# Seven-product multiplication with both running sums in one PSUM tile: product order, weight rounding and memory attention rearranged

## The chip, the cores and the metric

The kernel runs on one core of a Trainium2 chip. The metric is the time of one execution on the device in microseconds (us), and the lower the better. The kernel before takes 1235.52 us, the median of 3 runs (1234.53 to 1237.28).

## The reference

One layer of a hybrid streaming encoder, for a prompt of 512 tokens and a sample group of 32 tokens (544 rows in all), width 1024. The sample group attends to caches of 512 tokens. All in float32.

```
h = rms_norm(x, norm_mix)
q, k, v, xb, gb, qc = split(h @ w_in)                  # 1024 columns each
a_out = differential attention(q, k, v)                # 8 heads, two 64-wide maps each, 128-wide values
b_out = rglru(xb) * gelu(gb)                           # width-4 conv, block gates, linear recurrence
c_out = cross_attention(qc, mem_k, mem_v)              # 4 heads x 256, 256 memory tokens
gates = sigmoid(h @ w_gate + b_gate)                   # 3 x 1024 columns: ga, gb, gc
merged = gates_a * (a_out @ w_proj_a) + gates_b * (b_out @ w_proj_b) + gates_c * (c_out @ w_proj_c)
x = x + merged @ w_out
g_ff, u_ff = split(rms_norm(x, norm_ffn) @ w_ffn_in)   # 2816 columns each
x = x + (silu(g_ff) * u_ff) @ w_ffn_out
y = rms_norm(x, norm_final)
```

Before that, keys and values of the memory are made from `mem_prompt` (rms_norm and `w_mem_kv`). Besides y, the new keys and values, the memory's keys and values, and the states of the convolution and the recurrence are returned.

## The kernel before, in words

**Numbers.** Every product is made in float32r. A float32 value is split into a high part (rounded, `A(h_, src)` on ACT) and a low part (the difference, `LO` on DVE), for activations and weights alike. A product takes three passes: high weights with high and with low activations, low weights with high activations. Activations are transposed, 128 rows of the width on the partitions and 544 columns of tokens; 544 is taken as two halves of 272. PSUM is divided into two accumulators `acc` of two banks each and four `side` tiles of one bank each.

**Plain gemm** (`gemm`, L564): for 128 output rows all 8 blocks of 128 inputs, 48 matmuls of 272 columns (32 with the high weights, 16 with the low), into both banks of one `acc`.

**Seven products** (`seven`, L1820): 256 output rows and pairs of input blocks form a 2x2 scheme with seven products (A11, A12, A22, P1 to P4) instead of eight. It is used for the query of the memory attention (qc), for the gate products gb and gc, for one of ga, and for the whole first FFN matrix: 13 items of 256 columns before the FFN, 22 in it. One product is 12 matmuls of 272 columns. The running sum `a` stands in bank 0 of an `acc`, and its intermediate values are copied out by ACT between the products (`quarters`, L1869): after A11, after P2 and after P3. The next product into `a` may start when the copy has been made. The second sum `b` (P1, P4) and the single product A12 stand in a `side` tile each. The order is A11, [A22 and P4 of the item before], A12, P2, P1, P3; the last two products of an item are pending until the next item or gemm calls `flush` (L1842).

**Weights.** SP loads chunks of 1 MB, two ahead, `raw`. For the seven products, sums of weights are needed; one is added by a DMA with accumulation on POOL's queue, others by DVE (`raw<-raw`, L267). `split_blocks` (L487) issues roundings in the order of use.

**Order.** All instructions are issued at build time by a planner (`Flow`, L48). It keeps a time `fl.now` on PE and one of each engine by a cost per instruction; generators wait with `fl.get` for events and with `fl.take` for buffers, and instructions go into each engine's queue in the order of these planned times. Each engine then runs its queue in that order and waits for semaphores. The order of the weight chunks is written out by hand: `HEAD`, then `MID` (L360), where a name and a number are a chunk of 256 columns (x and g: recurrence and GeLU branch; ya, yb, yc: projections), "flush" and "cross" are marks where the main line waits, then w_out and the FFN (`FF_ORDER`).

**Memory attention** (`cross_kv` L1460, `cross` L1500): per head, keys and values come back from DRAM, go out to the result, and are split (buffers `mh`, `ml`, two each, both used by one head). Four row blocks of 128 queries each go through maximum, exponential, sum and division (`soft_rows`), then two pairs of blocks are transposed and multiplied with the values. The split queries `cq` have room for one head; a query's `t1` tile is free only when its split is made.

**Recurrence** (`x_evac` L1320, `g_evac` L1388, `scan` L1409): convolution, two gates, recurrence and GeLU, ten `L` tiles. A gate's result waits in `t1` (four of them), gb 2's and gb 3's in `L`, until its projection comes.

**Norm ahead of the FFN** (`row_norm`, L703): a sum of squares over the rows by small matmuls, an inverse root by DVE, a broadcast by small matmuls. The FFN's first products don't need it; their copies out of PSUM do.

Of the kernel before, what the change touches and what calls it, by code (L numbers as in the profile page):

```python
# [9 lines left out]
F32 = mybir.dt.float32  # L10
# [195 lines left out]
def hybrid_step(ctx: ExitStack, tc, io):  # L206
# [139 lines left out]
    def chunk(w, c, k0=0, nk=8):  # L346
# [130 lines left out]
    def split_plain(i, j):  # L477
        nk = chunks[i][1]
        for e in range(0, nk, 4):
            yield from split((i, j, e), raws[i][:, e:min(e + 4, nk), j * P:(j + 1) * P])  # L480
        ks = [((i, j, k // 4 * 4), k % 4) for k in range(nk)]
# [5 lines left out]
    def split_blocks():  # L487
# [4 lines left out]
        late = None  # L492
        for i in ORDER:
            if i == "flush":
                yield from late
                late = None
                continue
            yield from fl.get(("raw", i, 0))
            if i not in FAST:
                for j in range(2):  # L500
                    yield from split_plain(i, j)

                    if late is not None:
                        yield from late
                        late = None
# [6 lines left out]
            if late is not None:  # L512
                yield from late
# [3 lines left out]
            p2, a22, p1 = q[0], q[2], q[3]  # L517
            VT(p2, p1, q[0], OP.add)
            yield from split((i, "P2"), b4(p2))
            yield from split((i, "P1"), b4(p1))  # L520
            if aside is not None:
                yield from split((i, "P3"), b4(aside))
            else:
                yield from split((i, "A22"), b4(a22))
                VT(a22, p2, a22, OP.subtract)
                yield from split((i, "P3"), b4(a22))
            late = split_late(i, b4, a22, q[1], p2, aside)

    def split_late(i, b4, a22, a12, p2, aside):
        if aside is not None:  # L530
            yield from split((i, "A22"), b4(a22))
# [51 lines left out]
    def gemm(tiles, xh, xl, n=T, need=None):  # L583
# [18 lines left out]
        if need is None:  # L602
            for c, j, evac in tiles:
# [4 lines left out]
                yield from products(acc, c, j, [(0, b, k) for k in ks for b in range(2)], True, False)  # L608
# [46 lines left out]
    comb = tl(const, [P, 64], F32, "comb")  # L655
    onesm = tl(const, [P, P], F32, "onesm")
    ones_d = tl(const, [P, 1], F32, "ones_d")
# [7 lines left out]
    nlam = tl(const, [P, 1], F32, "nlam")  # L665
    sgn = tl(const, [P, 1], F32, "sgn")
    subg = tl(const, [P, 1], F32, "subg")
    bv = tl(const, [HEADS, REL_N], F32, "bv")
# [34 lines left out]
    def row_norm(pool, sqs, n, rb, ev, late=None):  # L703
# [6 lines left out]
        banks = len(blocks) if len(sqs) > 1 else 1  # L710
        yield from fl.take(*["side"] * banks)
# [13 lines left out]
        yield fl.when(y)  # L725
# [82 lines left out]
    def start_vecs(sp):  # L808
        yield from fl.get(("sent", 5))
        dma(comb, io["c_comb"], 32768)  # L810
# [7 lines left out]
        yield td + 1500  # L818
        yield from fl.take("side", "side")
# [29 lines left out]
    def softplus():  # L849
# [3 lines left out]
        mx, ab, ww, den, zz, z2, pl = (tl(const, [P, 8], F32, f"sp_{n}") for n in "mawdzyp")  # L853
# [80 lines left out]
    def mem_out():  # L934
# [4 lines left out]
        yield None  # L939
# [144 lines left out]
    def sample(at, p):  # L1084
# [25 lines left out]
        yield VS(cm, comb, st[:, 2:3], None, OP.mult)  # L1110
# [335 lines left out]

    def soft_rows(s_, e, free_side):
        i_st = S["cst n"] = S.get("cst n", -1) + 1
        st = S["cst"][:, 3 * i_st:3 * i_st + 3]
# [10 lines left out]
    def cross_kv(cr, h):  # L1460
        yield from fl.take("mraw", "mraw", "mh", "mh", "ml", "ml")
        res = []
        for src in (mk_d, mv_d):
            r = slot_tile(cr, [P, 2, 256], F32, "mraw")
            t = dma(r, src[h], 262144)
            res.append((r, t))
        outs = (io["o_mk"][h], io["o_mv"].rearrange("(t p) d -> p t d", p=P)[:, :, h * 256:(h + 1) * 256])
        for i, (r, t) in enumerate(res):
            yield t
            t_out = dma(outs[i], r, 262144)  # L1470
            hi = slot_tile(cr, [P, 2, 256], F32R, "mh")
            lo = slot_tile(cr, [P, 2, 256], F32R, "ml")
            yield VC(hi, r)
            t = LO(lo, r, hi)
            fl.give("mraw", max(t, t_out))
            S["mkv", h, i] = (hi, lo)
            fl.set(("mkv", h, i), t)

    def c_evac(cr, h):
        def go(c, a):  # L1480
# [3 lines left out]
            q = yield from quarters(c, new_t1, a, each, -1.0)  # L1484
# [13 lines left out]
        return lambda c, a: member("cross", go(c, a))  # L1498

    def cross(cr, h):  # L1500
# [6 lines left out]
        def rows(i):  # L1507
            yield from fl.take("ce", "side")
            s_ = side_tile()
            n = 0  # L1510
            for j in range(2):
                for a, b in ((q[j][0], mkh), (q[j][1], mkh), (q[j][0], mkl)):
# [726 lines left out]
```

## Time and profile before

| what | value |
|---|---|
| median of 3 runs | 1235.52 us |
| the profiled execution, its own time | 1239.9 us |
| its span, first to last instruction | 1238.1 us |
| TensorE matmul (PE) busy | 1182.8 us, 96% |
| VectorE (DVE) busy | 877.3 us, 71% |
| ScalarE (ACT) busy | 585.3 us, 47% |
| mean granted clock of TensorE | 0.982 |

The profile is of one execution, so sums are made against its own time. PE is the matmul engine, PEld its weight loads, which overlap. A matmul's end is modelled: one of 272 columns is shown as about 0.29 us long, while the next starts 0.125 us after it. An idle time in brackets stands in front of the instruction that waited, with the instruction that ended the wait.

### The profile page before, as it was taken

The page shows a single profiled execution, that of the slowest core. Times are in us where ns is not written, and L with a number is a line of the kernel's source. Part 1 is how long each engine was busy: PE and PEld are TensorE (multiplying, and loading weights), DVE is VectorE, ACT ScalarE, POOL GpSimd, SP SyncE. Part 2 cuts the span into 40 slices and gives each one's busy share as a digit, 9 for nine tenths or more (in the row PEclk, how much of TensorE's full clock was granted, in tenths as well). Part 3 has the DMA queues.
Part 4 walks back from the last instruction along what each step waited for, and adds up shares of the span by engine and source line. Part 5 has one row for each costly group of instructions (what it writes and reads, how often), then busy time and mean ns, then how long its engine had stood idle before and what let it go on. Part 6 is the DMA issues. An engine that isn't in the chain of part 4 may idle for free.

```text
span 1238.1 us, 23076 instructions
## 1 busy us (share of the span) xinstructions
PE 1182.8 (96%) x9200; PEld 1163.1 (94%) x9200; DVE 877.3 (71%) x1861; ACT 585.3 (47%) x1171; POOL 76.4 (6%) x145
## 2 busy tenths in 40 slices
PE   8999999999999997999999689998999999999996
PEld 8899999999999997999999689998999999999996
DVE  6886878786648885475878675578887757756755
ACT  5635454444325554353656653355455525524422
POOL 0002000000000000000111000010111011011001
PEclk9999999999999998999999899998999999999998
DMA  7682343321243443214223133343566556554322
GB/s 263 223 269 97 134 139 116 105 87 58 98 136 103 129 137 111 77 44 145 78 77 112 51 98 143 114 120 95 141 166 138 145 137 168 140 151 120 106 65 73
DMA packets 58875, 151.95 MB, mean 123 GB/s; under 512 B 6632, under 2 KB 18280, under 8 KB 52624
## 3 DMA queue, kind: packets, MB, share of 16 engines
q1 hardware_dynamic: 50560, 135.53, 32.7%
q0 software_dynamic: 8208, 14.95, 7.5%
q8 instruction: 72, 1.18, 0.4%
q14 instruction: 35, 0.29, 0.1%
HBM read 139.52 MB, written 13.68 MB: 124 GB/s over the span
## 4 chain that ended last, share of the span: by engine, by line
PE 85%; DVE 8%; ACT 4%; issue 2%; DMA 1%; SPq 0%; ACTq 0%; DVEq 0%
PE acc L327 65%; PE side L327 19%; DVE wl L267 3%; PE side L334 2%; ACT wh L254 1%; DVE raw L267 1%; DMA raw<-in_w_mem_kv 1%; ACT L L254 0%; ACT t L254 0%; DVE t L267 0%; DVE rst L267 0%; DVE fq L267 0%; DVE x L276 0%; DVE al L267 0%; ACT fq L254 0%
## 5 line engine op out<-in xcount | busy, mean ns | idle before, releaser
L254 ACT ACTIVATE wh<-raw 128x512 fp32r<-128x512 f32 (+2 forms) x357 | 234.5, 669 | 282.6 <-PE acc L327 124.6
L267 DVE TENSOR_TENSOR wl<-raw,wh 128x512 fp32r<-128x512 f32 (+2 forms) x358 | 260.7, 740 | 49.5 <-ACT wh L254 33.4
L327 PE MATMUL acc<-hh,wh 128*128 128x272 f32 x852 | 185.6, 291 | 0.0
L327 PE MATMUL acc<-hl,wh 128*128 128x272 f32 x852 | 184.3, 290 | 0.0
L327 PEld LDWEIGHTS acc<-hh,wh 128*128 128x128 f32 x852 | 137.9, 189 | 0.7 <-ACT fq L254 0.3
L327 PEld LDWEIGHTS acc<-hl,wh 128*128 128x128 f32 x852 | 137.5, 189 | 0.1
L327 PE MATMUL acc<-ah,wh 128*128 128x272 f32 x596 | 127.3, 288 | 0.0
L327 PE MATMUL acc<-al,wh 128*128 128x272 f32 x596 | 127.2, 288 | 0.0
L327 PE MATMUL acc<-hh,wl 128*128 128x272 f32 x852 | 124.7, 291 | 0.1
L327 PE MATMUL acc<-bh,wh 128*128 128x272 f32 (+2 forms) x416 | 98.1, 294 | 17.2 <-ACT t L254 14.5
L327 PEld LDWEIGHTS acc<-hh,wl 128*128 128x128 f32 x852 | 113.3, 189 | 0.6 <-DVE wl L267 0.4
L327 PE MATMUL acc<-bl,wh 128*128 128x272 f32 (+2 forms) x416 | 96.1, 289 | 0.0
L327 PEld LDWEIGHTS acc<-ah,wh 128*128 128x128 f32 x596 | 95.8, 189 | 0.0
L327 PEld LDWEIGHTS acc<-al,wh 128*128 128x128 f32 x596 | 95.5, 188 | 0.0
L327 PEld LDWEIGHTS acc<-bh,wh 128*128 128x128 f32 x416 | 71.5, 190 | 19.7 <-ACT t L254 16.7
L327 PE MATMUL acc<-ah,wl 128*128 128x272 f32 x596 | 84.1, 289 | 0.0
L327 PE MATMUL side<-hh,wh 128*128 128x272 f32 x296 | 77.7, 290 | 2.6 <-DVE t L267 2.1
L327 PEld LDWEIGHTS acc<-ah,wl 128*128 128x128 f32 x596 | 78.7, 189 | 0.0
L267 DVE TENSOR_TENSOR x<-acc,x 128x544 f32<-128x544 f32 (+2 forms) x43 | 29.3, 684 | 69.6 <-PE acc L327 69.6
L327 PE MATMUL side<-hl,wh 128*128 128x272 f32 x296 | 77.1, 288 | 0.0
L327 PEld LDWEIGHTS acc<-bl,wh 128*128 128x128 f32 x416 | 71.3, 190 | 0.0
L327 PE MATMUL acc<-bh,wl 128*128 128x272 f32 (+2 forms) x416 | 63.3, 290 | 0.0
(338 smaller groups left out, 2393.4 us busy)
## 6 DMA issues: line engine op xcount, KB each, us to landing
raw<-in_w_in SPq DMA_DIRECT2D x20, 1024.0 KB, 5.7
raw<-in_w_ffn_in SPq DMA_DIRECT2D x22, 512.0 KB, 4.3
raw<-in_w_ffn_in SPq DMA_DIRECT2D x44, 256.0 KB, 4.8
raw<-in_w_ffn_out SPq DMA_DIRECT2D x12, 768.0 KB, 4.2
raw<-in_w_mem_kv SPq DMA_DIRECT2D x7, 1024.0 KB, 6.5
fb<-in_w_ffn_in SPq DMA_DIRECT2D x22, 256.0 KB, 4.7
raw<-in_w_ffn_in POOLq DMA_DIRECT2D x22, 256.0 KB, 4.3
fb<-in_w_ffn_in POOLq DMA_DIRECT2D x22, 256.0 KB, 5.4
```

Source lines behind the costliest of these rows:

```text
L254: nc.scalar.activation(out, in_, func, scale=scale, bias=bias, accum_out=accum_out)
L267: nc.vector.tensor_tensor(out, a, b, o)
L327: nc.tensor.matmul(out, lhsT=lhsT, rhs=rhs, start=start, stop=stop, skip_group_check=shared)
L334: nc.tensor.transpose(out, in_, ident[:n, :n])
```

## The change

Six things are changed together.

1. `seven`, `flush`, `quarters`: both running sums `a` and `b` are the two banks of one `acc`, and only A12 has a `side` tile. The order is A11, [A22 of the item before], P2, [P4 of the item before], P1, P3, A12. `flush` takes one pending product or both; `gemm` calls it within its first tile after half of the high-weight matmuls and after all of them. The accumulator is given back after `b` has been read.
2. `split`: the rounding of a sum of weights is issued when its planned time of completion has come, not before. The splits come in the order of the products; without a second buffer the sum for P3 is made in P1's place.
3. `MID` has another order, and the gates' results have places by name (`HOLD`): gc 0, gc 3 and gb 1 in two new tiles `gt`, gb 2 and gb 3 in `L`.
4. Memory attention: row blocks go in pairs (one `side` tile and one maximum for two), keys and values have buffers of their own (`mhk`, `mlk`, `mhv`, `mlv`, one each), the high part is made by ACT, and the sample group has its own tile. The results o_mk and o_mv leave by copies from DRAM to DRAM, planned 150 us after the start of the attention stage.
5. yb 2 is one gemm of two tiles that takes the inputs as they come (`need`), yb 1 comes ahead of "lru", and the wait at the end of that stage is for n from 2 on.
6. `row_norm` ahead of the FFN issues its two groups of matmuls 2.5 us later each. Constants and the tiles of `softplus` go to other pools; four columns share one tile.

```diff
-    MID = [("qc", 0), ("ga", 3), ("qc", 1), ("qc", 2), ("qc", 3), ("gc", 0), ("gc", 1), "flush", "cross",
-           ("yc", 0), ("gc", 2), ("x", 0), ("yc", 1), ("gc", 3), ("yc", 2), ("g", 0), ("x", 1), ("yc", 3), "bh", ("g", 1),
-           ("gb", 0), ("x", 2), ("g", 2), ("x", 3), ("g", 3), ("gb", 1), ("gb", 2), ("gb", 3), ("yb", 2), "mh", ("yb", 3),
-           "lru", ("yb", 0), ("yb", 1)]
+    MID = [("qc", 0), ("qc", 1), ("gc", 0), ("qc", 2), ("qc", 3), ("ga", 3), ("gc", 1), ("gc", 2), "flush", "cross",
+           ("yc", 0), ("x", 0), ("gc", 3), ("yc", 1), ("g", 0), ("x", 1), ("yc", 2), ("yc", 3), "bh", ("g", 1),
+           ("x", 2), ("g", 2), ("x", 3), ("gb", 0), ("g", 3), ("gb", 1), ("gb", 2), ("gb", 3), ("yb", 2), "mh", ("yb", 3), ("yb", 1),
+           "lru", ("yb", 0)]
+    HOLD = {("gc", 0): "gt", ("gc", 3): "gt", ("gb", 1): "gt", ("gb", 2): "L", ("gb", 3): "L"}
...
     def split(name, src):
         yield from fl.take("hb", "lb")
+        if fl.when(src) > fl.now:
+            yield fl.when(src)
...
             yield from split((i, "A11"), b4(q[0]))
-            if late is not None:
-                yield from late
-            yield from split((i, "A12"), b4(q[1]))
+            if late:
+                yield from late.pop(0)
...
             VT(p2, p1, q[0], OP.add)
             yield from split((i, "P2"), b4(p2))
+            if late:
+                yield from late.pop(0)
             yield from split((i, "P1"), b4(p1))
...
+            if aside is None:
+                VT(p1, p2, a22, OP.subtract)
+            yield from split((i, "P3"), b4(p1 if aside is None else aside))
+            yield from split((i, "A12"), b4(a12))
+            late += [split((i, "A22"), b4(a22)), split_last(i, b4, a12, p2, aside)]
...
                 ks = range(chunks[c][1])
-                yield from products(acc, c, j, [(0, b, k) for k in ks for b in range(2)], True, False)
+                yield from products(acc, c, j, [(0, b, k) for k in ks[:4] for b in range(2)], True, False)
+                yield from flush(0)
+                yield from products(acc, c, j, [(0, b, k) for k in ks[4:] for b in range(2)], False, False)
+                yield from flush(1)
...
+        yield fl.now + later
         yield from fl.take(*["side"] * banks)
...
-        yield fl.when(y)
+        yield fl.when(y) + later
```

The new `seven` and `flush`:

```
        a, b = acc[:, 0, :HT], acc[:, 1, :HT]
        fl.spawn(evac(c, a, b))
        yield from product(a, c, "A11", forms, True, False)
        yield from flush(0)
        yield from fl.get(("c11", c))
        yield from product(a, c, "P2", forms, False, False)
        yield from flush(1)
        yield from fl.get(("c12", c))
        yield from product(b, c, "P1", forms, True, False)
        yield from product(a, c, "P3", forms, False, False)
        yield from fl.take("side")
        S["c", c] = c_ = side_tile()[:, :HT]
        yield from product(c_, c, "A12", forms, True, True)
        S["pending"] += [(c, a, "A22", forms), (c, b, "P4", forms)]

    def flush(*which):
        for w in which or (0, 1):
            if len(S["pending"]) == 2 - w:
                c, dst, form, forms = S["pending"].pop(0)
                yield from fl.get(*((("u3", c), ("c22", c)) if w == 0 else (("a4", c),)))
                yield from product(dst, c, form, forms, False, True)
```

The new row pairs and the buffers of memory attention:

```
            for i in range(2):
                n = 0
                for j in range(2):
                    for a, b in ((q[j][0], mkh), (q[j][1], mkh), (q[j][0], mkl)):
                        MM(s_[:, i * NMEM:(i + 1) * NMEM], a[:, (2 * qp + i) * P:(2 * qp + i + 1) * P], b[:, j], n == 0, n == 5)
                        n += 1
...
            nc.vector.tensor_reduce(st[:, 0:2], sv, AX.X, OP.max)
...
declare(mraw=1, mhk=1, mlk=1, mhv=1, mlv=1, cq=4, ce=2, ces=1, pth=1, ptl=1, ck=1, cv=1, qs=2, pts=1)
...
            if item == ("yb", 2):
                yield from gemm([(i, j, ev(2 * c + j)) for j in range(2)], xh, xl, need=lambda k: ("b", k))
                continue
```

## Rows read from the trace of the kernel before

**Rows 1.** The page's busy times by engine.
```profile
PE 1182.8 (96%) x9200; PEld 1163.1 (94%) x9200; DVE 877.3 (71%) x1861; ACT 585.3 (47%) x1171; POOL 76.4 (6%) x145
```

**Rows 2.** Busy time by stage; stretch, its length, then engines, clock, DMA.
```profile
core 0: us, PE busy (x) PEld busy (x) DVE busy (x) ACT busy (x) POOL busy (x), PEclk, DMA share, GB/s
63.00:297.00 234.00, 234.00 (x1843) 228.75 (x1842) 179.22 (x547) 107.86 (x258) 7.45 (x22) 1.00 0.39 131
...
371.00:480.00 109.00, 104.65 (x814) 102.52 (x812) 88.51 (x204) 60.33 (x140) 5.15 (x6) 0.98 0.45 131
480.00:497.00 17.00, 11.42 (x58) 9.74 (x57) 9.52 (x26) 5.03 (x13) 0.00 (x0) 0.80 0.09 34
497.00:686.00 189.00, 185.65 (x1470) 184.77 (x1469) 132.06 (x216) 99.58 (x190) 15.73 (x54) 1.00 0.28 90
686.00:748.00 62.00, 46.97 (x338) 45.64 (x337) 41.67 (x70) 39.39 (x71) 2.65 (x7) 0.89 0.23 73
...
838.00:850.00 12.00, 7.83 (x47) 7.52 (x46) 10.98 (x30) 6.08 (x11) 0.00 (x0) 0.72 0.04 7
850.00:1166.00 316.00, 311.13 (x2437) 306.31 (x2437) 227.81 (x407) 148.61 (x295) 34.94 (x40) 1.00 0.55 145
```

**Rows 3.** Waits over the whole span: us in total, times, longest.
```profile
ACT wh L254 <- DVE raw L267: 120.8, 57, 8.9
...
PE acc L327 <- ACT t L254: 16.6, 9, 8.0
```

**Rows 4.** Timeline of PE in the FFN: start us, length, engine, what.
```profile
1017.39 0.28 PE L327 MATMUL side<-hh,wh 128*128 128x272 f32 x1
...
1019.09 0.39 PE L327 MATMUL acc<-hh,bh 128*128 128x272 f32 x1
...
1025.60 1.16 PE L327 MATMUL acc<-m,wh 128*128 128x272 f32 x8
...
1030.11 0.29 PE L327 MATMUL acc<-hh,wh 128*128 128x272 f32 x1
```

**Rows 5.** Timeline of ACT in the same stretch.
```profile
1018.12 0.63 ACT L254 ACTIVATE wh<-raw 128x512 fp32r<-128x512 f32 x1 [3.88 <-DVE raw L267]
1018.66 0.38 ACT L254 ACTIVATE fq<-acc 128x272 f32<-128x272 f32 x1
...
1025.80 0.40 ACT L254 ACTIVATE t<-acc 128x272 f32<-128x272 f32 x1 [1.11 <-PE acc L327]
```

**Rows 6.** Waits of PE and PEld in the FFN, 850 to 1166 us.
```profile
PE acc L327 <- ACT t L254: 2.1, 2, 1.1
PE acc L327 <- ACT fq L254: 1.6, 3, 0.7
...
PEld acc L327 <- ACT fq L254: 4.2, 10, 0.9
PEld acc L327 <- ACT t L254: 3.3, 5, 1.3
```

**Rows 7.** Timeline of ACT, PE and DVE at the end of memory attention.
```profile
464.55 0.39 ACT L254 ACTIVATE t<-acc 128x272 f32<-128x272 f32 x1
...
465.00 0.40 PE L327 MATMUL acc<-bh,wh 128*128 128x272 f32 x1 [2.24 <-ACT t L254]
...
480.56 0.42 DVE L283 CAST mh<-mraw 128x512 fp32r<-128x512 f32 x1
```

**Rows 8.** Timeline of ACT and PE at gb 1.
```profile
703.21 0.63 ACT L254 ACTIVATE wh<-raw 128x512 fp32r<-128x512 f32 x1 [2.30 <-DVE raw L267]
...
704.73 0.60 PE L327 MATMUL acc<-bh,wh 128*128 128x272 f32 x1 [8.02 <-ACT t L254]
...
707.61 0.43 PE L327 MATMUL side<-bh,wh 128*128 128x272 f32 x1
```

**Rows 9.** Timeline of DVE in the yb projections.
```profile
759.79 0.72 DVE L276 SCALAR_TENSOR_TENSOR L<-L,acc 128x544 f32<-128x544 f32 x1 [2.21 <-PE acc L327]
```

**Rows 10.** Timeline of DVE at the norm ahead of the FFN.
```profile
846.06 0.43 DVE L267 TENSOR_TENSOR al<-fq,ah 128x272 fp32r<-128x272 f32 x1
```

More of the change, by code (lines that the diff above doesn't have):

```diff
@@ L480, in split_plain @@
             yield from split((i, j, e), raws[i][:, e:min(e + 4, nk), j * P:(j + 1) * P])
+            if between:
+                yield from between.pop(0)
+        while between:
+            yield from between.pop(0)
         ks = [((i, j, k // 4 * 4), k % 4) for k in range(nk)]
@@ L1571, in cross_sample @@
         yield from fl.get(("cq", h, 0), ("cq", h, 1))
-        yield from fl.take("ce", "side")
+        yield from fl.take("ces", "side")
         sx = side_tile()[:, :NMEM]
@@ L1674, in fast_tanh, with go @@
     def fast_tanh(br, c):
-        own = br == 1 and c >= 2
+        tag = HOLD.get(("g" + "abc"[br], c), "t1")
         def new():
-            yield from fl.take("L")
-            return l_tile(S["lr"])[:, :T]
+            if tag == "t1":
+                return (yield from new_t1())
+            yield from fl.take(tag)
+            return slot_tile(S["lr"], [P, 552], F32, "L")[:, :T] if tag == "L" else slot_tile(S["gp"], [P, T], F32, "gt")
         def bias(j):
             return bgh[:, br * 8 + 2 * c + j:br * 8 + 2 * c + j + 1]
-        def go(i, a):
+        def go(i, a, b):
             def each(g, j, cs, src):
@@ L1688, in each @@
                     yield A(g[:, cs], src, AF.Tanh, scale=0.5 if cs.start else -0.5, bias=bias(1))
-            g = yield from quarters(i, new if own else new_t1, a, each, -1.0)
+            g = yield from quarters(i, new, a, b, each, -1.0)
             t = A(g[0], g[0], AF.Tanh, scale=0.5, bias=bias(0))
@@ L1697, in go @@
                 S["gate", br, n] = g[j]
-                S["gate tag", br, n] = "L" if own else "t1"
+                S["gate tag", br, n] = tag
                 fl.set(("gate", br, n), fl.when(g[j]))
@@ L1894, in quarters @@
         yield from each(t1, 1, hi, t1[:, hi])
+        yield from fl.get(("done", c, "A12"))
+        t = VT(t0[:, lo], S["c", c], t0[:, lo], OP.add)
+        fl.give("side", t)
+        yield t
+        yield from each(t0, 0, lo, t0[:, lo])
         yield from fl.get(("done", c, "A22"))
         yield from each(t1, 1, lo, a)
-        give_acc(fl.when(t1[:, lo]))
+        fl.set(("a4", c), fl.when(t1[:, lo]))
         yield from fl.get(("done", c, "P4"))
         t = VT(t0[:, hi], b, t0[:, hi], OP.add)
-        fl.give("side", t)
+        give_acc(t)
         yield t
@@ L1914, in each @@
                     VT(g[:, cs], src, S["rb"][:, cs], OP.mult)
-            g = yield from quarters(c, new, a, each)
+            g = yield from quarters(c, new, a, b, each)
             S["fg", i, n] = g
@@ L1957, in ffn_in @@
             yield from between
-        yield from flush()
     def fo_evac(fp, i, n):
@@ L2099, in main @@
         mid = iter(MID)
-        with tc.tile_pool(name="cross", bufs=1, reuse_waits="tile") as cr:
-            S["cr"] = cr
-            declare(mraw=2, mh=2, ml=2, cq=4, ce=4, pth=1, ptl=1, ck=1, cv=1, qs=2, pts=1)
-            S["cst"] = tl(cr, [P, 60], F32, "cst")
-            ch = tl(actp, [P, KD, T], F32R, "ah")
-            cl = tl(actp, [P, KD, T], F32R, "al")
-            yield from after_attention(mid)
-            yield idle("cross")
-            yield from fl.get(*[("cs", h) for h in range(4)], *[("c", h, qp) for h in range(4) for qp in range(2)])
```

244 lines of the change are left out of this document (114 added, 130 removed).

## The prediction

> **What bounds the kernel now.** I read the page first: TensorE (PE) is busy 1182.8 of 1238.1 us [rows 1], so no other engine's load sets the time; what can be won is what PE loses. The change adds no matmul and takes none away, so the question is only which PE stalls go and which come. Next I read the table by stage [rows 2]. A stage's loss is its idle time plus (1 - clock) x length, since the granted clock has two levels, 1.2 and 2.4 GHz, and a mean of 0.80 means that part of the stretch ran at the lower one. That gives: 371-480 us 4.35 + 2.2, 480-497 us 5.58 + 3.4 (memory attention, with the query and gate products, 15.5 together); 497-686 us 3.35, 686-748 us 15.03 + 6.8 (recurrence and gates, 25.2 together); 838-850 us 4.17 + 3.4 (second norm, 7.5); 850-1166 us 4.87 (FFN). The reader is to see that these sum to 53, that the pairs' stage (63-297 us) loses nothing, and that three short stretches hold most of it.
>
> The waits [rows 3] name the culprit: PE waits longest for ScalarE (ACT) copies, and ACT itself stands 120.8 us, 57 times, in roundings of weights whose sum VectorE (DVE) has not made. A copy issued behind such a rounding is late, as one shows [rows 4 to 5]: the first product of an item ends at 1017.39, its copy starts only at 1018.66, behind the rounding of 1018.12 that came after 3.88 us of waiting for the sum. The copy ends at 1019.04 and PE goes on at 1019.09. An undisturbed copy stands beside it: product over at 1025.60, copy 1025.80 to 1026.20. So a copy that nothing delays holds PE up 0.20 + 0.40 + 0.05 = 0.65 us if PE has nothing else to do.
>
> **The change, part by part.** A product is 1.50 us: 1025.60 to 1030.11 are three of them [rows 4].
>
> *Order of the seven products, sums in two banks of one tile.* There are 35 such items, 22 of them in the FFN. In the old order the first copy (after A11) has three products as cover, 4.5 us; the second (after P2) and third (after P3) have one, 1.5 us. In the new order the first has one (A22 of the item before), the second two (P4, P1), the third two (A12, next A11): cover of 1.5, 3.0, 3.0. One thin spot instead of two. But where no item is pending, P2 follows A11 with no cover at all, 0.65 us each: qc 0, gc 3, gb 0, gb 1 and the first item of each of three FFN groups. Every later product stands behind P2 in PE's queue, so these are paid in full.
>
> *Rounding only when the sum is made.* The planner now issues the rounding at the time it reckons the sum ready, so copies get in front. In the FFN this should remove nearly every wait of PE for ACT. Its size lies between 3.7 us (the matmuls' waits, 2.1 + 1.6) and 7.5 us (the weight loads' waits for the same copies, 4.2 + 3.3) [rows 6]; I take 6.0, above the middle, because a stall also costs the overlap with the matmul before it (1.50 / 12 = 0.125 apart, shown as 0.28 long [rows 4]). Less two uncovered starts at 0.65 (the third is in the norm's stage): **FFN -4.7** (from -6.2 to 0, the latter if ACT is held as before and the thinner cover eats the rest).
>
> *Memory attention.* Two things hold PE. At 465.00 it waits 2.24 us for a copy which ACT makes at 464.55, behind the query splits: the gate's tile waited for a t1 buffer that the last head's query still held. And in the tail, 480-497 us, PE has only the last head's chain; it starts with the keys' rounding at 480.56, which could not begin while the head before still had its buffers [rows 7]. After the change keys and values have buffers of their own, the keys' free after the second row pair; gc 0 and gc 3 have tiles of their own; and gc 2's 7 x 1.50 = 10.5 us of products stand ahead of "cross", where 9.0 us are lost now. I let 6.0 of the 15.5 remain, because the chain row sums, transposes, products stays serial: -9.5, and +0.65 for qc 0: **-8.8** (from -14.9 to +0.65, the latter if the tail only starts later). Row pairs make 16 row maxima into 8, and the keys' and values' rounding goes from DVE to ACT; both lie beside PE work (ACT 60.33, DVE 88.51 of 109 us [rows 2]), priced at nothing. If that cover went, one rounding (0.63 [rows 5]) would stand before a head's first row, at most 4 x 0.63 in all.
>
> *Gates and recurrence.* The largest single wait is 8.02 us at 704.73: gb 1's second product waits for the first copy [rows 8]. ACT was in a line of recurrence work and then stood 2.30 us in a weight rounding at 703.21; and the copy needed a t1 buffer that the last GeLU tiles held. Now gb 1 has a tile that is free, its rounding no longer blocks, and gb 0's 10.5 us lie between the last x and the last g product. But ACT's recurrence work is all still there, and gb 0 meets it with no cover. Between "all 25.2 stay" and "all go" no row decides; I take half, -12.6, plus three uncovered starts (gc 3, gb 0, gb 1), +1.95: **-10.6** (from -23.2 to +16.8, the third rival).
>
> *yb 2 as one two-tile gemm.* gb 3's item is still pending and holds one of two accumulators, and it is flushed only in yb 3. So yb 2's two halves and yb 3 share the other one, and PE waits twice for an evacuation that another accumulator hides now: 0.20 + 0.72 + 0.05 each, the 0.72 from the DVE evacuation [rows 9]: **+1.9** (from 0, if gb 3's DVE work fits, to +1.9).
>
> *The norm's matmuls 2.5 us later, twice.* PE would not wait for the sum of squares. But the input that the first FFN product needs, al from fq, is itself written only at 846.06 [rows 10], and the new order asks for the later forms (P2, P1) right after A11, uncovered. So most of the 7.5 stays: **-1.0** (from -7.5 to +1.3, two uncovered waits).
>
> *Priced at nothing:* the outputs of memory keys and values now leave in the pairs' stage, eight transfers on SP's queue in front of weight loads. PE idles 0.00 of 234 us there with DMA engines at 0.39 [rows 2], so weights arrive early. Comb, the small constants and softplus's tiles only change pools. If the cover were gone, a late weight tile would show as waits of PE for DMA in 200-297 us, where there is none.
>
> **Sum.** -4.7 - 8.8 - 10.6 + 1.9 - 1.0 = -23.2 us. The profiled execution took 1239.9 us (span 1238.1 and 1.8 around it), 4.4 above the median of 1235.5; there the change should give 1216.7, at the median 1212.3.
>
> **A rule that speaks against it.** The FFN has some fifteen waits of up to 1.3 us [rows 6] with the granted clock at 1.00 throughout [rows 2], so short stalls of this kind have not lowered it.
> The Trainium skill (page "TensorE: Matmul & The Clock Gate", section "A second HAM failure mode: psum-queue depth-cycling") says that PE idling briefly and often between groups of matmuls as it goes through PSUM banks can be enough to swing its clock between both levels; the uncovered starts would be such idles. By the trace the sum stays; by the rule it is the fifth case below.
>
> **The rivals.**
> 1. *The stalls move rather than go.* The tail of memory attention starts 10.5 us later with half its length won (-4 instead of -9.5), the recurrence stage gives 4 instead of 12.6, the rest as forecast: 1212.3 + 5.5 + 8.6 = 1226. For it: the order is fixed by a planner whose costs have missed stalls of 8 us. Against: the largest two each have a named buffer that the change frees.
> 2. *All goes:* cross -13, gates -20 + 2, FFN -6.2: 1212.3 - 4 - 7.4 - 1.5 = 1199. Against it: the serial chains stay.
> 3. *Slower: gb 0 behind the last x product.* Its first copy stands uncovered behind ACT's recurrence line. If PE waits 8.0 us there and the clock falls as it did (6.8), and gb 1's wait stays, the stage loses 14.8 more instead of 12.6 less, +16.8 with the starts: 1212.3 + 10.6 + 16.8 = 1240. It decides from a loss in gb 0 and gb 1 together of some 23 us more than forecast. For it: ACT is busy 39.39 of 62 us there [rows 2]. Against: ACT stood idle behind weight sums in that very line.
> 4. *The rounding rule does nothing,* since it goes by planned, not real time: FFN 0 and 5 us more in the two earlier stages, 1222.
> 5. *The clock falls at uncovered starts:* a product at the lower level took 2.88 us (704.73 to 707.61 [rows 8]) against 1.50, so 7 x 1.4 more: 1222.
>
> **How the numbers follow.** Forecast 0.52 (1203 to 1223), first rival 0.19, second 0.12, slower 0.11, fourth 0.03, fifth 0.03. The likeliest gives 1212. Leaving out about a tenth on either side, the range is 1196 to 1237: below lies the unlikely half of the second case, above the slower one. A difference of 0.2% (2.5 us) is what can be told from none here. Faster than that: all but the slower case and the end of the first, 0.84; within 0.05; slower 0.11.
>
> **What would show it.** Right: ACT's waits for weight sums fall from 120.8 to below 40; PE's waits for ACT in the FFN below 2 us except about 0.65 at each group's start; no wait at gb 1 over 2 us; the stretch from the last gate's flush to yc 0 below 10 us; two waits of about 1 us around yb 2. Wrong: PE waiting for the first copy in most items (the cover of 1.5 us too thin), several us at gb 0, a tail of 15 us after gc 2, or PE waiting for weights, which would mean that the later roundings starve it.

## The result and the profile after

The changed kernel takes 1277.15 us (median of 4 runs, 1275.03 to 1277.68) against 1235.74 in the runs beside it: ratio 1.0331, interval 1.0313 to 1.0349. It is slower by 41 us; I had forecast 1212 and a range that ended at 1237.

Busy times of the page, after. The amount of PE work is the same (x9200); PE is busy 14.7 us longer than in [rows 1], in a span that is 37.8 us longer.

```profile
PE 1197.5 (94%) x9200; PEld 1170.9 (92%) x9200; DVE 876.5 (69%) x1828; ACT 591.6 (46%) x1180; POOL 75.7 (6%) x145
```

Busy time by stage, after, in the columns of [rows 2].

```profile
370.00:498.00 128.00, 124.32 (x982) 121.98 (x981) 100.26 (x210) 76.96 (x175) 5.15 (x6) 1.00 0.38 112
498.00:690.00 192.00, 184.70 (x1440) 182.64 (x1440) 138.34 (x223) 110.47 (x206) 15.12 (x55) 0.99 0.26 85
690.00:748.00 58.00, 48.74 (x374) 47.04 (x374) 36.47 (x61) 26.46 (x49) 2.54 (x6) 1.00 0.28 96
...
823.00:835.00 12.00, 7.47 (x37) 6.41 (x37) 10.63 (x29) 6.36 (x12) 0.00 (x0) 0.74 0.00 0
835.00:1240.00 405.00, 367.35 (x2732) 356.24 (x2732) 253.81 (x444) 159.43 (x312) 34.94 (x40) 0.97 0.45 120
```

Memory attention now loses 3.7 us, where [rows 2] gave 15.5, and the recurrence and gates lose 18.5 (7.3 + 1.9 and 9.3 + 0) instead of 25.2. Counted in matmuls these two stretches won less than the 18.5 us by which the losses differ: 2796 in 378 us, where the rows of before have 2680 in 377, which at 0.125 us each is 13.5 us. The FFN is the news: 37.65 us idle in 405 and a clock of 0.97, where the rows of before had 4.87 in 316 and 1.00. One row stands for the split, the write of the input that the first FFN product needs, in DVE's timeline after; ahead of it here, the last write of x before the norm:

```profile
823.03 0.72 DVE L267 TENSOR_TENSOR x<-acc,x 128x544 f32<-128x544 f32 x1 [2.47 <-PE acc L327]
...
828.32 0.43 DVE L267 TENSOR_TENSOR al<-fq,ah 128x272 fp32r<-128x272 f32 x1
```

It came at 846.06 before [rows 10]. So the kernel is 17.7 us ahead there, and from there to the end takes 447.6 us (1275.9 - 828.32) instead of 392.0 (1238.1 - 846.06): 55.5 us lost after a gain of 17.7. By the last write of x, 838.39 us before, the lead is 15.4 us; the other 2.4 come from the norm's small DVE steps, which stood ahead of the row at 846.06 and now come behind the one at 828.32.

The waits, after, say for what. PE's waits for copies, 16.6 us for t alone in [rows 3], are down to 3.8 + 4.8 + 2.9, and ACT's waits for weight sums have fallen from 120.8 to 70.7 us (my sign of being right was below 40); now PE waits for rounded weights. In the FFN's rows raw and fb are loaded weights, wh and bh their rounded high parts, wl and bl the low parts; t, fq and gt are copies of a running sum.

```profile
ACT wh L254 <- DVE raw L267: 70.7, 39, 5.5
...
PE acc L327 <- ACT wh L254: 24.7, 20, 2.6
...
PE acc L327 <- ACT gt L254: 4.8, 5, 1.9
PE acc L327 <- ACT t L254: 3.8, 6, 1.6
...
PE acc L327 <- ACT fq L254: 2.9, 6, 0.5
...
PE acc L327 <- DVE L L276: 1.8, 2, 0.9
```

One FFN item shows how. Timelines after, of PE, DVE, ACT, SP and POOL in that order; a last bracket is the idle time before, with its releaser.

```profile
911.35 0.66 PE L327 MATMUL acc<-m,wl 128*128 128x272 f32 x4
913.86 0.46 PE L327 MATMUL acc<-hh,wh 128*128 128x272 f32 x1 [1.85 <-ACT wh L254]
...
912.05 0.44 DVE L276 SCALAR_TENSOR_TENSOR t<-acc,fq 128x272 f32<-128x272 f32 x1 [1.75 <-PE acc L327]
912.40 0.68 DVE L267 TENSOR_TENSOR raw<-raw 128x512 f32<-128x512 f32 x1
913.84 0.69 DVE L267 TENSOR_TENSOR wl<-raw,wh 128x512 fp32r<-128x512 f32 x1 [0.76 <-ACT wh L254]
914.45 0.68 DVE L267 TENSOR_TENSOR raw<-raw 128x512 f32<-128x512 f32 x1
915.89 0.69 DVE L267 TENSOR_TENSOR wl<-raw,wh 128x512 fp32r<-128x512 f32 x1 [0.76 <-ACT wh L254]
...
913.18 0.63 ACT L254 ACTIVATE wh<-raw 128x512 fp32r<-128x512 f32 x1 [2.23 <-DVE raw L267]
915.23 0.63 ACT L254 ACTIVATE wh<-raw 128x512 fp32r<-128x512 f32 x1 [1.42 <-DVE raw L267]
...
901.86 0.33 SPq L318 DMA_DIRECT2D raw<-in_w_ffn_in  x1
916.61 0.80 SPq L318 DMA_DIRECT2D raw<-in_w_ffn_in  x2
...
907.46 0.86 POOL L426 DMA_DIRECT2D raw<-in_w_ffn_in  x1 [12.45 <-DMA raw<-in_w_ffn_in]
```

PE ends A22 of the item before and stands still for 1.85 us until P2's weights are there. In front of them lie, one after another, the read of a (912.05), the sum for P2 (912.40), its rounding (913.18): the sum stands behind the read in DVE's queue, and the read waits for A22. The order of the instructions also makes a loop. SP can load the next chunk only when a load buffer comes back, that is after P4's piece of the item before: sum 914.45, rounding 915.23, low part 915.89 to 916.58, next load 916.61. Its piece stands behind P2's sum of this item. This needs the adding DMA (issued 907.46; this group's median landing on the page is 4.3 us later, so about 911.8), and it stands behind the read of a (912.05), for which A11 and A22 must be done. Either way begins when the plain loads issued from 901.86 have landed. One turn takes 14.75 us (901.86 to 916.61); the seven products take 10.5. Over eight turns the mean is 14.7 us, before it was 12.3. In this stretch it was 11.3, as SP's timeline of that kernel shows:

```profile
898.74 0.33 SPq L318 DMA_DIRECT2D raw<-in_w_ffn_in  x1
...
910.00 0.33 SPq L318 DMA_DIRECT2D raw<-in_w_ffn_in  x1
```

Of the two, the read of a was the later by a little. POOL, which issues the adding DMA, waits for the plain loads each time; beside it only DVE waits for these loads, and briefly, as the waits after, 835 to 1200 us, show:

```profile
DVE raw L267 <- DMA raw<-in_w_ffn_in: 0.6, 2, 0.4
```

### The profile page after: what moved, and what is told of

The parts are those of the page before. It is cut to its first block, busy times and chain, and to the rows that moved or that the text cites. A ratio compares the mean times of both kernels' runs of the same rounds, so it can differ in the third digit from the quotient of the medians.

```text
span 1275.9 us, 23045 instructions
## 1 busy us (share of the span) xinstructions
PE 1197.5 (94%) x9200; PEld 1170.9 (92%) x9200; DVE 876.5 (69%) x1828; ACT 591.6 (46%) x1180; POOL 75.7 (6%) x145
## 4 chain that ended last, share of the span: by engine, by line
PE 83%; DVE 9%; ACT 4%; DMA 2%; issue 2%; DVEq 0%; SPq 0%; ACTq 0%
PE acc L327 70%; PE side L327 11%; DVE wl L267 2%; PE side L334 2%; DVE raw L267 1%; ACT wh L254 1%; DMA raw<-in_w_mem_kv 1%; DMA raw<-in_w_ffn_in 1%; DVE bl L267 1%; DVE al L267 0%; DMA raw<-in_w_proj_b 0%; ACT L L254 0%; DVE L L276 0%; ACT bh L254 0%; DVE t L267 0%
## 5 line engine op out<-in xcount | busy, mean ns | idle before, releaser
L327 PE MATMUL acc<-hh,wh 128*128 128x272 f32 x1028 | 241.1, 299 | 29.6 <-ACT wh L254 19.7
L327 PE MATMUL acc<-hl,wh 128*128 128x272 f32 x1028 | 235.5, 294 | 0.0
L327 PEld LDWEIGHTS acc<-hh,wh 128*128 128x128 f32 x1028 | 175.2, 193 | 37.1 <-ACT wh L254 23.9
L327 PEld LDWEIGHTS acc<-hl,wh 128*128 128x128 f32 x1028 | 175.2, 193 | 0.1
L327 PE MATMUL acc<-hh,wl 128*128 128x272 f32 x1028 | 156.9, 294 | 0.0
L327 PEld LDWEIGHTS acc<-hh,wl 128*128 128x128 f32 x1028 | 141.5, 193 | 0.3 <-DVE wl L267 0.2
L327 PE MATMUL acc<-bh,wh 128*128 128x272 f32 (+2 forms) x464 | 111.1, 294 | 9.2 <-ACT gt L254 3.3
L327 PE MATMUL acc<-bl,wh 128*128 128x272 f32 (+2 forms) x464 | 109.1, 290 | 0.0
L327 PEld LDWEIGHTS acc<-bh,wh 128*128 128x128 f32 x464 | 80.6, 190 | 11.8 <-ACT gt L254 4.2
L327 PEld LDWEIGHTS acc<-bh,wl 128*128 128x128 f32 x464 | 63.4, 190 | 3.0 <-DVE wl L267 3.0
L254 ACT ACTIVATE t<-acc 128x272 f32<-128x272 f32 (+1 forms) x70 | 29.8, 425 | 68.8 <-PE acc L327 68.6
```

Source lines behind the costliest of these rows:

```text
L254: nc.scalar.activation(out, in_, func, scale=scale, bias=bias, accum_out=accum_out)
L327: nc.tensor.matmul(out, lhsT=lhsT, rhs=rhs, start=start, stop=stop, skip_group_check=shared)
```

## The experiments

Times are medians; each ratio is to the kernel before, timed on the same chip beside it. What holds for several kernels is said behind the last of them.

**Order of the pieces, and holding the roundings.** `late_first` rounds both pending pieces right after A11, so that P4's piece, and with it the load buffer, no longer waits for P2's sum:

```diff
             yield from split((i, "A11"), b4(q[0]))
-            if late:
+            while late:
                 yield from late.pop(0)
```

> The changed kernel (1277 us) with one thing undone: both pending pieces of the weights of an item (A22's and P4's) are rounded right after A11's of the next item, before the wait for the DMA that adds onto the weights. Theory A, buffer loop: in the changed kernel a weight buffer comes free only after P4's piece, which stands behind the sum of the next item, which waits for the adding DMA; the loop load 5.6 + adding DMA 4.3 + sums, roundings and differences 4.9 takes 14.75 us per item against 10.5 us of products. Undone, the loads start about 5 us earlier and the FFN needs 400 to 410 us instead of 452: 1222 us (1212 to 1235). Theory B, roundings held back until the planned time starve PE: no change, 1270 or more. Theory C, the copies out of the shared tile hold PE: no change, 1270 or more.

Measured: 1238.13 us, ratio 1.002 (1.0004 to 1.0035). 39 of the 41 us are back with one word; it is still above my range, which ended at 1235. A turn of the loads takes 12.4 us in the mean of eight. PE's waits after it:

```profile
PE acc L327 <- ACT wh L254: 10.3, 9, 1.6
```

`no_hold` takes the rounding rule out of the changed kernel:

```diff
-        if fl.when(src) > fl.now:
-            yield fl.when(src)
```

> The changed kernel with the rounding rule undone: a rounding is issued as before, without waiting for the planned end of its sum. Theory A (buffer loop): the order of the pieces and the loop stay, so 1265 to 1285 us, no gain. Theory B (held-back roundings starve PE): the FFN comes back to about 400 us, 1225 to 1240. Theory C (copies out of the shared tile): slower by some us, as copies stand behind blocked roundings again, 1280 or more.

Measured: 1284.34 us, ratio 1.0386 (1.0359 to 1.0414). 7 us longer: held roundings don't starve PE. The other two theories both had this time in their range, so the run doesn't choose between them.

`before_hold` is the kernel before with these two lines and nothing else of the change.

> The kernel before with only the rounding rule of the change added (a rounding waits for the planned end of its sum). My prediction's step: copies get in front of blocked roundings, PE's waits for ACT in the FFN go, about -6 us there and a few elsewhere: 1228 us (1222 to 1234). Theory B (held-back roundings starve PE): 1245 or more. Theory A says nothing against the first.

Measured: 1226.2 us, ratio 0.9923 (0.9896 to 0.9949). 9.2 us gained.

**What closes the loop.** `no_add_dma` leaves the two adding DMAs of each first-FFN chunk out, but not their time in the plan:

```diff
-                nc.gpsimd.dma_start(b[:, 1536:], d[:, 1536:], accum_op=OP.add)
-                if aside:
-                    nc.gpsimd.dma_start(xb, d[:, :512], accum_op=OP.add)
+                if not aside:
+                    nc.gpsimd.dma_start(b[:, 1536:], d[:, 1536:], accum_op=OP.add)
```

> The changed kernel without the two adding DMAs of each first-FFN weight chunk (two sums of weights are left out, so the FFN's values are not the reference's); the planner's times and order stay. Theory A (buffer loop): the loop loses 4.3 us, 14.75 to about 10.4, just under the 10.5 of the products, so most of the FFN's 42 us of waits for weights go: 1228 us (1218 to 1242). Theories B and C: nothing changes, 1270 or more.

Measured: 1270.76 us, ratio 1.0286 (1.0258 to 1.0313), a gain of 6.4. My first reading, that the transfer itself holds the loop, falls; a turn still takes 14.5 us. `no_add_plan` tells the planner too:

```diff
-                fl.set(("raw", i, 1), t + 4000)
+                fl.set(("raw", i, 1), t if aside else t + 4000)
```

> The changed kernel without the two adding DMAs of each first-FFN chunk (its sums lack what they add), as in no_add_dma, but now the planner too is told that the last part of the chunk is there when its plain loads have landed, not 4.0 us later. Theory A' (the 1.85 us wait ahead of P2 is written into the planned order: P4's piece, and with it the return of the load buffer, stands behind the next item's P2 sum, whose planned time waits for the adding DMA; the sum is therefore issued on DVE behind the evacuation of the running sum a, which on the chip waits for A22' directly in front of P2): with an earlier planned sum the loop is 4.0 us shorter than the 14.8 us seen, so close to the 10.5 us of products, and most stalls go: 1235 us (1222 to 1246). Rival R1 (the planned time does not matter, the buffer's return behind the next item alone starves PE): no change against no_add_dma, 1270 us (1264 to 1275).

Measured: 1252.5 us, ratio 1.0115 (1.0093 to 1.0136): another 18 us, though outside the range expected (1222 to 1246); a turn takes 13.2 us. PE's waits of `no_add_dma` and of `no_add_plan`:

```profile
PE acc L327 <- ACT wh L254: 24.1, 21, 2.5
```

```profile
PE acc L327 <- ACT wh L254: 13.8, 15, 1.2
```

With the transfer gone the waits stay as they were, and the sum still stands behind the read of a. DVE and PE in `no_add_dma`:

```profile
905.88 0.44 DVE L276 SCALAR_TENSOR_TENSOR t<-acc,fq 128x272 f32<-128x272 f32 x1 [1.77 <-PE acc L327]
906.24 0.68 DVE L267 TENSOR_TENSOR raw<-raw 128x512 f32<-128x512 f32 x1
...
907.70 0.40 PE L327 MATMUL acc<-hh,wh 128*128 128x272 f32 x1 [1.85 <-ACT wh L254]
```

The waits halve only when the planned time moves. So most of the 1.85 us was the place in the instruction order that the planner gave P2's sum, behind the read of a, and the smaller part the transfer. What is left in `no_add_plan` stands one product later: 12 waits of 1.00 us ahead of P4 of the item before. Its sum is made behind P2's low part, and its rounding stands behind the copy of a, for which P2 must be done (ACT, then PE):

```profile
919.02 0.40 ACT L254 ACTIVATE t<-acc 128x272 f32<-128x272 f32 x1 [2.34 <-PE acc L327]
919.32 1.14 ACT L254 ACTIVATE wh<-raw 128x512 fp32r<-128x512 f32 x2
...
919.99 0.40 PE L327 MATMUL acc<-hh,wh 128*128 128x272 f32 x1 [1.00 <-ACT wh L254]
```

`late_first`, 14 us faster, makes that piece ahead of P2's and has none of these waits. What the buffer's return costs beside them was not tried by itself. A third load buffer, which might open the loop without any reordering, wasn't tried either.

**The tile that both sums share.** `late_own_bank` is `late_first` with b in a tile of its own:

```diff
-        a, b = acc[:, 0, :HT], acc[:, 1, :HT]
+        a = acc[:, 0, :HT]
+        yield from fl.take("side")
+        b = side_tile()[:, :HT]
...
+        give_acc(fl.when(t1[:, lo]))
...
-        give_acc(t)
+        fl.give("side", t)
```

The last lines belong to it: an accumulator that holds a alone is given back when a has been read, one that holds both only when b has been read.

> The changed kernel with both pending pieces rounded right after A11 (as late_first), and with b, the second running sum, in a PSUM tile of its own instead of the second half of a's tile; the order of the products stays. Theory C (a wait is taken on the whole tile, so P1 into b waits for the copy of a, and P4' into b for the read of a after A22', 0.5 to 1.0 us each): of the 14 us that late_first's FFN is longer in waits than before_hold's (26.5 against 12.8 us) most comes back, and some in the gates: 1226 us (1220 to 1231). Rival R2 (the order of the products costs it, P2 and P1 each right behind a read, whatever tile b lies in): 1237 us (1234 to 1241).

Measured: 1221.91 us, ratio 0.9864 (0.9838 to 0.989): 16 us, for the waits on the tile and the earlier return together, which no run parts. `own_bank` makes the same edit in the changed kernel, whose pieces stay as they are:

> The changed kernel with b in a PSUM tile of its own and nothing else: the order of the pieces, the order of the products and the planned wait of P4' for the read of a stay. If the order of the pieces and the shared tile are two causes (A'): 1277 us less the 16 us that the own tile gave on late_first, 1261 us (1254 to 1267), and the 1.8 us stalls ahead of P2 stay in most FFN items. Rival R9 (the shared tile is at the root of both): 1228 us (1220 to 1240), and those stalls are gone.

Measured: 1261.02 us, ratio 1.0183 (1.0153 to 1.0213), and PE's waits show the old stalls:

```profile
PE acc L327 <- ACT wh L254: 24.7, 13, 4.2
```

So it is two causes that add: 16 us for the tile with either order of the pieces, 39 us for the order with either tile (1277 to 1238, 1261 to 1222). `own_bank_free` also lets P4' go as soon as its sum is there:

```diff
-                yield from fl.get(*((("u3", c), ("c22", c)) if w == 0 else (("a4", c),)))
+                yield from fl.get(*((("u3", c), ("c22", c)) if w == 0 else (("c22", c),)))
```

> own_bank, and the pending P4' no longer planned behind the read of a after A22' but behind the sum it needs (c22), as in the kernel before. If the order of the pieces alone holds the load buffers (A'): no change against own_bank, 1261 us (1254 to 1267). Rival R10 (the planned wait makes the plan late and so the buffers): 1240 us (1225 to 1250).

Measured: 1263.53 us, ratio 1.0211 (1.0186 to 1.0236): no gain, so that planned wait held nothing.

**The rest of the change without the new products.** `front_only` is the changed kernel with pieces, products, flushes and yb 2 as before (the old text of `split_blocks`, `seven`, `quarters`, `flush` and `gemm`, and b in its own tile).

> The changed kernel with the products, their weight pieces and the two running sums as in the kernel before (P1 and b in a tile of their own, A22' and P4' in one go), yb 2 as before; the rounding rule, the memory attention in row pairs, the order of gates and recurrence, the gate buffers and the later norm stay. Theory A' (what is lost is lost by the order of pieces and products, the front parts gain on their own): 1226.2 us of before_hold less the 8.8 us of the memory attention and some 5 of the 10.6 of gates and recurrence, that is 1212 us (1205 to 1219). Rival R3 (the 14.7 us that the changed kernel is ahead at the norm come from the new order of products and the bank that it frees): 1225 us (1221 to 1230).

Measured: 1211.26 us, ratio 0.9781 (0.9762 to 0.9801). It beats both kernels. Its FFN, and PE's longest waits:

```profile
826.00:1192.00 366.00, 363.72 (x2865) 359.67 (x2865) 259.39 (x462) 166.58 (x326) 34.99 (x40) 1.00 0.49 133
```

```profile
PE acc L327 <- DVE wl L267: 5.5, 2, 4.0
PE acc L327 <- ACT wh L254: 5.3, 5, 2.4
```

The FFN loses 2.28 us in 366. `front_shared_tile` puts b into a's tile again, in the old order of products, with the return of the accumulator that goes with it, and changes nothing else:

```diff
+        S["b", c] = b = acc[:, 1, :HT]
...
-        yield from fl.take("side")
-        S["b", c] = b = side_tile()[:, :HT]
...
-        give_acc(fl.when(t1[:, lo]))
...
-        fl.give("side", t)
+        give_acc(t)
```

> front_only with b in the second half of a's PSUM tile and nothing else; the order of the products stays that of the kernel before. It asks for the price of the shared tile alone. Theory C (the wait is taken on the whole tile): P1 waits for the copy of a behind P2, 0.46 us in each of 35 items as in late_own_bank's gain, 16 us; P4', right behind A22', also waits for the read of a where that read stands ahead of it, another 0.5 to 1.0 us each: 1240 us (1224 to 1262). Rival R8 (in this order A12 and the second pending product cover both): 1213 us (1210 to 1217).

Measured: 1264.09 us, ratio 1.0221 (1.0202 to 1.0239). The shared tile costs 53 us here, a little more than the range expected (to 1262). PE and ACT at one P1 of it:

```profile
904.84 0.29 PE L327 MATMUL acc<-hh,bh 128*128 128x272 f32 x1
904.97 0.29 PE L327 MATMUL acc<-hl,bh 128*128 128x272 f32 x1
905.74 0.39 PE L327 MATMUL acc<-hh,bh 128*128 128x272 f32 x1 [0.49 <-ACT t L254]
...
905.29 0.40 ACT L254 ACTIVATE t<-acc 128x272 f32<-128x272 f32 x1 [0.91 <-PE acc L327]
```

Two matmuls of P1 have gone into b when the copy of a is reached in the program; the copy waits for them, and the next matmul into b waits for the end of the copy (905.29 + 0.40, then 905.74), though the two sums lie in different halves of the tile. The wait is taken on the tile, not on the half. Between 850 and 1190 us PE waits 34 times for a copy or a read of a when some matmuls into b have gone, 17 us in all; how much of the rest comes from the later return of the accumulator is not shown.

**Three smaller terms.** `late_yb_plain` is `late_first` with yb 2 as two ordinary products (the three lines of the `need` form out).

> The changed kernel with both pending pieces rounded right after A11 (as late_first), and with yb 2 as two ordinary products that take up the pending A22' and P4' on the way, instead of the form that goes by the hidden branches that are ready and holds the pending pair's accumulator. If my price for that accumulator holds (1.9 us), and the other waits of 748 to 838 us (8.0 us in late_first against 0.7 in the kernel before) come from it too: 1232 us (1229 to 1236). Rival R4 (these waits come from the recurrence and gate order, not from the accumulator): 1238 us (1236 to 1241), or longer, since the products then wait for hidden branches in a fixed order.

Measured: 1235.01 us, ratio 0.9977 (0.9965 to 0.9989), 3.1 below `late_first` (5 by the two ratios). The term was there, larger than its price of 1.9: PE's waits of 0.90, 0.91 and 1.72 us at 727 to 742 us of `late_first` are gone. The waits around it did not go with it. `late_pair` is `late_own_bank` with that edit and both pending products ahead of P2:

```diff
-        yield from flush(0)
+        yield from flush()
         yield from fl.get(("c11", c))
         yield from product(a, c, "P2", forms, False, False)
-        yield from flush(1)
```

> late_own_bank with two more edits: the pending A22' and P4' both run ahead of P2 (A11, A22', P4', P2, P1, P3, A12), and yb 2 as two ordinary products. What is left of the new order is that A12 comes last. Theory A'' (in late_own_bank P2 is the next thing behind A22', so its weights, which wait for the adding DMA, are late by up to 1.56 us; a second product ahead of P2 covers them): of the 10.7 us between late_own_bank and front_only most comes back: 1215 us (1210 to 1219). Rival R5 (A12 last is what costs, because P2 loses the cover of A12 whatever else stands there): 1221 us (1219 to 1225).

Measured: 1218.32 us, ratio 0.9856 (0.9843 to 0.987), in its range but with 3.6 of the 10.7 us, half of what was hoped, and the edit of yb 2 in it had given 3.1 by itself. 850 to 1190 us in `late_own_bank` and in `late_pair`:

```profile
850.00:1190.00 340.00, 331.13 (x2612) 328.73 (x2612) 233.90 (x418) 149.27 (x292) 31.37 (x36) 1.00 0.49 133
```

```profile
850.00:1190.00 340.00, 337.12 (x2679) 336.02 (x2678) 237.69 (x422) 151.67 (x296) 31.52 (x36) 1.00 0.50 132
```

and PE's longest wait over the whole of `late_pair`, by total and by single wait:

```profile
PE acc L327 <- ACT t L254: 8.4, 6, 5.5
```

In the FFN the second product ahead of P2 takes the idle time from 8.87 to 2.88 us, so A12 last costs next to nothing there. What is left stands elsewhere, 5.5 us of it in one wait at the first FFN items (at 843 us).

`front_no_hold` and `front_norm_early` take one more step each out of `front_only`, the rounding rule and `later=2500`.

> front_only without the rounding rule (a weight sum's rounding is again queued on ACT before the sum is made). The rule was worth 9.2 us on the kernel before; if it acts on the roundings of every seven-product item, whatever stands around them: 1220 us (1216 to 1224). Rival R6 (with the new memory attention and gates ACT has less to be held by, and only the 5 us of the FFN are left): 1216 us (1213 to 1218).

Measured: 1231.0 us, ratio 0.9964 (0.9952 to 0.9976).

> front_only with the norm ahead of the FFN planned as in the kernel before (its two steps not held back by 2.5 us). The step was priced at 1.0 us of gain: 1212.3 us (1211.5 to 1214). In the traces the norm's second wait on PE was 2.26 us in the kernel before and 0.83 us in front_only, which would make it 1.4 us. Rival R7 (a wait of the same length stands elsewhere): 1211.3 us, no difference that can be measured.

Measured: 1210.05 us, ratio 0.9788 (0.9775 to 0.9801). The rule is worth 20 us there, twice what it is worth on the kernel before and more than the range expected (to 1224); the later norm is worth nothing that can be measured.

## Why the prediction was wrong, by its steps

**The step that failed is "Order of the seven products, sums in two banks of one tile".** With the rounding rule it gave the FFN -4.7 us; from the row at 828.32 to the end it was +55.5. It priced the new order by the cover of the copies alone and left out two things: the order of the weights' pieces, worth 39 us, and the waits on the shared tile, worth 16. By the same row in the profiled runs, the 55.5 us are 43.2 for the pieces (447.6 to 404.3 in `late_first`, 1234.0 - 829.66), 3.6 for the tile (to 400.8 in `late_own_bank`, 1221.2 - 820.43), and 8.7 more to the 392.0 of before. The larger part of the tile's price between these two, 9.2 us, stands ahead of that row (829.66 to 820.43).

- *The weights' side of the order.* I followed PE's queue past the moved products, and not ACT's, DVE's and SP's past the moved pieces. In the diff P4's piece moved from ahead of this item's sum to behind it. That this order costs 39 us is shown by `late_first` and `own_bank`; that the planned time counted for more than the transfer, by `no_add_dma` and `no_add_plan`. That the load buffer, which comes back with P4's piece, closes the loop is argued and not shown: the wait in front of the sum for P2 is for the read of a. My list of signs had "PE waiting for weights", but blamed it on the held roundings: `no_hold` refutes that.
- *The covers were not what I listed.* "1.5, 3.0, 3.0" counted P1 as cover of the second copy. P1 goes into the other half of the tile that is being copied, so it waits for the copy. After, the first FFN group shows it on PE and ACT:

```profile
832.77 1.11 PE L327 MATMUL acc<-hh,wl 128*128 128x272 f32 x4
834.37 0.59 PE L327 MATMUL acc<-hh,wh 128*128 128x272 f32 x1 [0.49 <-ACT fq L254]
...
833.91 0.40 ACT L254 ACTIVATE fq<-acc 128x272 f32<-128x272 f32 x1 [3.18 <-PE acc L327]
```

In the FFN waits on the tile stand only at the starts of its three groups, where no P4 is pending (0.49 us each), and at their ends (0.97 to 0.98). Ahead of it they are longer, as one shows (the wait for the same copy is 0.67 us in `own_bank`):

```profile
524.77 0.48 PE L327 MATMUL acc<-bh,wh 128*128 128x272 f32 x1 [1.90 <-ACT gt L254]
```

The other terms came near in their sum. Up to the row at 828.32 the forecast was -8.8 - 10.6 + 1.9 - 1.0 = -18.5 us, measured -17.7, or -15.4 by the last write of x. That this is so near is luck in part: the tile, for which I had nothing, costs 8.1 us there (`own_bank` has the row at 820.20), so the other parts gained more than I gave them. The terms:

- *Memory attention*, -8.8: 3.7 instead of 15.5 lost, -11.8. Cheaper than the 6.0 that I let remain.
- *Gates and recurrence with yb 2*, -10.6 + 1.9: 18.5 instead of 25.2, -6.7, with a part of the tile's price in it. gb 1's 8.02 us are gone. The two waits priced for yb 2 are in the waits after, 0.9 us each (L from L276); the third that went in `late_yb_plain` I had not seen.
- *The norm*, -1.0: 7.7 us lost (4.53 + 0.26 x 12) where 7.5 were; `front_norm_early`, too, finds nothing gained.
- *The rounding rule*, -6.0 in the FFN and a part of the stages ahead: -9.2 alone, -19.7 in `front_only`. The sign held; the size depends on what stands around it. The fourth rival (it does nothing) is out.

`front_only`, which has all of these but yb 2, and not the failed step, takes 1211 us. That this is near my 1212 is partly chance: the rule gave more and the failed step was forecast at +1.3.

The third rival had the right sign, 1240, but another place: gb 0 and gb 1 do not carry the loss. The first and second fall with the FFN. The fifth I had tied to starts of 0.65 us; of the "fifteen waits" set against it, the matmuls had five by [rows 6]; fifteen is the number of the weight loads' waits. The clock did fall in the FFN, to a mean of 0.97 over 405 us, in the changed kernel, whose stalls there are 1.8 us and more; `front_shared_tile` idles often and briefly, and holds 1.00:

```profile
850.00:1190.00 340.00, 315.37 (x2411) 304.54 (x2411) 224.23 (x401) 147.55 (x289) 33.23 (x38) 1.00 0.49 129
```

There 24.6 us of 340 are idle, 22 of them in 42 waits of 0.48 to 0.62 us: the 34 on the tile and 8 for weights.
The Trainium skill (page "TensorE: Matmul & The Clock Gate", section "A second HAM failure mode: psum-queue depth-cycling") would let such brief and frequent idles between PSUM banks swing the clock; this trace does not agree, with its 1.00.

What stays open is some 7 us between `late_pair` and `front_only`. Both have the row that stands for the split at the same time (819.16 and 819.25), so they are lost behind it, most of them in the wait at 843 us; whether the new order of products costs them or the plan happened to fall worse no run tells.

## What to carry to other kernels

When work is reordered, follow the order on every queue that feeds it, and ask of each moved piece what now stands ahead of it, and which buffer it gives back. Two accumulators in one PSUM tile are one thing to the waits, so an instruction that fills one half is no cover for a read of the other. A mixed change is worth taking apart: of this one, the parts around the headline edit gained 2.2% and the headline edit lost more than that.

## What was not expected of the hardware

42 stalls of 0.48 to 0.62 us in 340 us left the granted clock at 1.00, and so did four stalls of 1.56 us in `late_first` (1.00 from 900 to 1200 us), while stalls of about 1.85 us in 12 of the 22 items went with 0.97 over the FFN. Behind the one shown above, PE's matmuls start 0.225 us apart (granted clock 0.51 from 914.0 to 917.3 us, the lower level), and from 917.50 on 0.125 apart again (1.00 to 920.0, the upper one):

```profile
914.57 0.43 PE L327 MATMUL acc<-hl,wh 128*128 128x272 f32 x1
914.80 0.43 PE L327 MATMUL acc<-hh,wh 128*128 128x272 f32 x1
...
917.50 0.29 PE L327 MATMUL acc<-hh,wh 128*128 128x272 f32 x1
917.62 0.29 PE L327 MATMUL acc<-hl,wh 128*128 128x272 f32 x1
```

PE's busy time per matmul does not give the price of that: it is 0.134 us in the changed kernel's FFN (367.35 / 2732) and 0.127 in `front_only` (363.72 / 2865), but 0.131 in `front_shared_tile` too (315.37 / 2411), at a clock of 1.00.

Taking 44 adding DMAs out of the queue of POOL, issued 4.3 and 5.5 us (medians) before they land, gave 6.4 us only, while a time written into the plan gave 18.
